# A projection by seven products: sums kept in PSUM banks, two scan levels made a step earlier, and branch B's gate path moved

## The chip, the core and the metric

The kernel runs on one core of one Trainium2 chip. The time is device microseconds of one execution; 1358.66 us is the median of three runs, which lie between 1352.6 and 1362.07. The core's engines work side by side, each through its own queue in order: PE (matmuls; its weight loads are shown as PEld), VectorE (DVE), ScalarE (ACT), GpSimd (POOL) and SyncE (SP), which issues nearly all DMAs. PE writes to eight PSUM banks; here a `[P, 512]` tile of float32 is one bank.

## What is computed

One inference step of one layer for 128 context and 1024 latent tokens (1152 in all) of width 1024. All matmuls of weights are made in three parts (high x high, high x low, low x high) to keep float32 precision.

```python
proj = h @ w_in
q, ff, fb, vi, zA, u, zB, gA, gB = jnp.split(proj, SPLITS, axis=-1)
...
logf_f, k_f = forget_gate(heads(ff), lb_f)
logf_b, k_b = forget_gate(heads(fb), lb_b)
o_f, S_f = hgrn2_chunk_scan(qh, logf_f, k_f, vh, s0_f)
o_b_rev, S_b = hgrn2_chunk_scan(qh[:, ::-1], logf_b[:, ::-1], k_b[:, ::-1], vh[:, ::-1], s0_b)
o = o_f + o_b_rev[:, ::-1]
o = o * lax.rsqrt(jnp.mean(o * o, axis=-1, keepdims=True) + EPS)
o = o * gnorm_w.reshape(N_HEADS_A, HEAD_V)
yA = o.reshape(B, L, D_A) * jax.nn.silu(zA)

yF = jnp.fft.fft2(ug, axes=(1, 3), norm='ortho').real.reshape(B, L, D_B)
yB = yF * jax.nn.silu(zB)
merged = jax.nn.sigmoid(gA) * (yA @ w_pa) + jax.nn.sigmoid(gB) * (yB @ w_pb)
return merged @ w_o, S_f, S_b
```

The scan is `S_t = diag(f_t) S_{t-1} + k_t v_t^T`, `o_t = S_t^T q_t`, for 8 heads and both directions. The context's final states are an output; the latents start from given states.

## The kernel before

**Stages.** From 0 to 174 us: normalisation, modulation, the first gate columns and half of the value projection. From 174 to 887 us: the other projections, as 27 calls of `pair`. From 887 to 1200 us: the scans of 8 heads, with late value columns and then the projection of the branches (`dense`) as filling. Then the last of those products and the output projection.

**`pair` (L613).** One call makes two blocks of 128 output columns for all 1152 tokens by a scheme with seven products instead of eight: `mov[i]` are seven sets of token operands (the halves `h1`, `h2` and the sums `tm`), `w[i]` seven weights, made of the four blocks a11, a21, a12, a22 of `raw` by four sums on VectorE (`sa`). Each weight is cast on ScalarE and its rest taken on VectorE or POOL (`split`). For each half j of 288 columns every product gets a PSUM bank of its own (`any_ps`, six banks in turn) and 12 matmuls, and VectorE forms the results by seven adds (L634) on `m1`, a copy by ScalarE (L647), through `u1`, `u2`, `u3`. `evac` applies the gate function, and a DMA stores the result. `raw` is one buffer, so the next pair's weights are fetched when the last reader is done.

**`four`.** Between products `next(four)` makes a step of other work: `fourier` (4 groups), then `pieces`, which prepares the scan: for each of 16 pieces of a head (640 or 512 tokens), levels of 1, 2 and 4 tokens. A level copies what it needs to `k0` and `q` (`halves`, ScalarE), multiplies `kk`, `qq` and `ff` by the decay (`grow`, VectorE, L461 and L463), makes 32x32 products of tokens (`within`, PE, L481) and merges them. `px` holds `ff` and `qq`, `pz` holds `kk`, `q` and `k0`; both have one buffer, and the next piece is loaded after the last level.

**Scans.** `PATTERN` (L53) has a row for each step n and writes down by hand the order in which parts are emitted: E is `scan_blocks(n)` (levels 8 and 16 of head n), L is `scan_rest(n - 1)` (levels 32 and 64, transposes of `kk`, state, read-out and scaling of the head before), Y the last part of the head before that, F a product of `dense`, V one of the late value columns. Matmuls of this stage are tied to that order (`queued`). All other instructions, and all of the stages before, are ordered by a scheduler when the program is built; each engine then runs its queue in order.

The order of the pairs is written out: two for u, 16 for the heads, seven for gates (`g_dr`), and last two for zB (`silu_fourier`), which need the Fourier result `yf` in tiles that take the place of `px` and `pz`. Then head 0 is loaded into the same place (`load_head`).

Of the kernel before, what the change touches and what calls it, by code (L numbers as in the profile page):

```python
# [11 lines left out]
F32 = mybir.dt.float32  # L12
# [3 lines left out]
ALU = mybir.AluOpType  # L16
# [50 lines left out]
def diffusion_step(ctx: ExitStack, tc: tile.TileContext, xT, x_tok, w_pr, w_v, w_ada, w_ada_gt,  # L67
# [134 lines left out]
    def mm3(out, pairs, mm=nc.tensor.matmul, first=True, last=True):  # L202

        n = len(pairs)
        for i, (sh, sl_, mh, ml) in enumerate(pairs):
            mm(out, lhsT=sh, rhs=mh, start=first and i == 0, stop=False)  # L206
            mm(out, lhsT=sh, rhs=ml, start=False, stop=False)  # L207
            mm(out, lhsT=sl_, rhs=mh, start=False, stop=last and i == n - 1)  # L208
# [350 lines left out]
    def pieces():  # L559
# [6 lines left out]
        def load(hd, t0, t1):  # L566
            w = t1 - t0
            nc.sync.dma_start(x[:, 0, :2 * w].rearrange("p (d t) -> p d t", d=2), f_dr[hd, :, :, t0:t1])
            nc.sync.dma_start(z[:, 1, :w], q_dr[hd, :, t0:t1])

        load(*todo[0])
        for i, (hd, t0, t1) in enumerate(todo):
# [10 lines left out]
            for m in (0,) + EARLY:  # L583
                if m:
                    halves(kk, k0, m, w)
                    halves(qq, q, m, w)
                    grow(ff, kk, qq, m, w)
# [3 lines left out]
                if m == EARLY[-1]:  # L591
                    nc.scalar.copy(fa, ff.rearrange("p (d t) -> p d t", d=2)[:, :, 0:w:GRAN])
                    nc.sync.dma_start(kk_dr[hd, :, :, t0:t1], kk.rearrange("p (d t) -> p d t", d=2))
                    nc.sync.dma_start(qq_dr[hd, :, :, t0:t1], qq.rearrange("p (d t) -> p d t", d=2))
                    nc.sync.dma_start(fa_dr[hd, :, :FA].rearrange("p (d t) -> p d t", d=2)[:, :, t0 // GRAN:t1 // GRAN], fa)
                    nc.sync.dma_start(fa_dr[hd, :, FA + t0 // P * 32:FA + t1 // P * 32], sm_[:, :n * 32])
                    if i + 1 < len(todo):
                        load(*todo[i + 1])
                yield
# [3 lines left out]
    with pool("se", 1) as se, pool("sl", 1) as sl_, pool("sp", 1) as sp:  # L603

        def split(src, tag):
            p = sl_ if tag in ("a12", "a22", "s4") else sp
            hi, lo = (p.tile([P, 4, P], F32R, name=tag + x) for x in "hl")
            nc.scalar.copy(hi, src)  # L608
            eng = nc.vector if tag[0] == "s" else nc.gpsimd
# [3 lines left out]
        def pair(n, evacs):  # L613
# [4 lines left out]
            sa = sp.tile([P, 4, P], F32, name="sa")  # L618
            (a11, a21), (a12, a22) = [[raw[:, 4 * d:4 * d + 4, i * P:(i + 1) * P] for i in range(2)] for d in range(2)]
            w = {1: split(a11, "a11")}  # L620
            nc.vector.tensor_tensor(out=sa, in0=a21, in1=a22, op=ALU.add)  # L621
            w[5] = split(sa, "s1")
            nc.vector.tensor_tensor(out=sa, in0=sa, in1=a11, op=ALU.subtract)
            w[6] = split(sa, "s2")
            nc.vector.tensor_tensor(out=a21, in0=a11, in1=a21, op=ALU.subtract)
            w[7] = split(a21, "s3")
            w[2] = split(a12, "a12")
            w[4] = split(a22, "a22")
            nc.vector.tensor_tensor(out=sa, in0=a12, in1=sa, op=ALU.subtract)
            w[3] = split(sa, "s4")  # L630
            mov = {1: h1[:4], 2: h1[4:], 3: h2[4:], 4: tm[3], 5: tm[0], 6: tm[1], 7: tm[2]}

            def add(out, x, m):
                nc.vector.tensor_tensor(out=out, in0=m, in1=x, op=ALU.add)  # L634

            for j in range(2):
                js = slice(j * SW, (j + 1) * SW)
                m = {}
                for i in (1, 5, 6, 7, 4, 2, 3):
                    m[i] = any_ps()[:, :SW]  # L640
                    mm3(m[i], [(w[i][0][:, k, :], w[i][1][:, k, :], mov[i][k][0][:, js], mov[i][k][1][:, js])
                               for k in range(4)])
                    if i in (() if n < 3 else (5, 4) if n < 8 else (5, 7, 2)):
                        next(four, None)
                m1, u1, u2, u3 = (se.tile([P, SW], F32, name=x) for x in ("m1", "u1", "u2", "u3"))
                ca, cb = (se.tile([P, 2, SW], F32, tag="c", name="c", bufs=3) for _ in range(2))
                nc.scalar.copy(m1, m[1])  # L647
                add(u1, m1, m[6])
                add(u2, u1, m[7])
                add(cb[:, 1], u2, m[5])  # L650
                add(u3, u1, m[5])
                add(ca[:, 0], m1, m[2])
                add(cb[:, 0], u2, m[4])
                add(ca[:, 1], u3, m[3])
                for c, (evac, dst) in zip((ca, cb), evacs):
# [50 lines left out]
        for _ in four:  # L706
            pass
# [450 lines left out]
```

## Time and profile before

| | |
|---|---|
| median of 3 runs | 1358.66 us (1352.6 to 1362.07) |
| profiled execution | 1363.05 us, span 1361.3 us, granted PE clock 0.971 |
| busy share of the span | PE 93%, PEld 87%, DVE 68%, ACT 44%, POOL 35% |
| matmuls | 12768 |

A line of the profile names the line of the code, the engine, the operation and the tiles as out<-in. Idle time in front of an instruction is put down to what released it. A wait "PE x <- DVE y" means that PE stood still, with all that is queued behind, until VectorE's instruction y had ended. "issue" is time for which the profile shows no release.

### The profile page before, as it was taken

The page shows a single profiled execution, that of the slowest core. Times are in us where ns is not written, and L with a number is a line of the kernel's source. Part 1 is how long each engine was busy: PE and PEld are TensorE (multiplying, and loading weights), DVE is VectorE, ACT ScalarE, POOL GpSimd, SP SyncE. Part 2 cuts the span into 40 slices and gives each one's busy share as a digit, 9 for nine tenths or more (in the row PEclk, how much of TensorE's full clock was granted, in tenths as well). Part 3 has the DMA queues.
Part 4 walks back from the last instruction along what each step waited for, and adds up shares of the span by engine and source line. Part 5 has one row for each costly group of instructions (what it writes and reads, how often), then busy time and mean ns, then how long its engine had stood idle before and what let it go on. Part 6 is the DMA issues. An engine that isn't in the chain of part 4 may idle for free.

```text
span 1361.3 us, 31510 instructions
## 1 busy us (share of the span) xinstructions
PE 1260.5 (93%) x12768; PEld 1183.7 (87%) x12768; DVE 922.2 (68%) x1639; ACT 601.3 (44%) x1168; POOL 470.0 (35%) x359
## 2 busy tenths in 40 slices
PE   5899799999999898999999899978999889999998
PEld 3679799999998898899999899977888788999886
DVE  7737755545468878889878787547767676565554
ACT  4542223433445455555554444334655555532332
POOL 4516523142422212122111111632422254455564
PEclk7899899999999999899999999989999899999999
DMA  8542233334445445454554456474776655567342
GB/s 321 197 171 71 66 128 102 132 130 133 134 136 164 148 162 161 155 182 140 179 203 137 166 183 210 142 285 149 236 240 225 217 184 153 169 202 224 113 138 98
DMA packets 126164, 227.54 MB, mean 167 GB/s; under 512 B 15537, under 2 KB 78786, under 8 KB 121794
## 3 DMA queue, kind: packets, MB, share of 16 engines
q1 hardware_dynamic: 125730, 224.47, 49.4%
q8 instruction: 100, 1.64, 0.5%
q10 hardware_dynamic: 288, 1.05, 0.3%
q14 instruction: 46, 0.38, 0.1%
HBM read 153.64 MB, written 71.84 MB: 166 GB/s over the span
## 4 chain that ended last, share of the span: by engine, by line
PE 28%; DMA 9%; DVE 7%; issue 3%; ACT 3%; POOL 2%; SPq 1%; DVEq 0%; ACTq 0%; POOLq 0%
PE d_ps L197 6%; PE o_ps L197 5%; DMA raw<-in_w_pr 3%; PE o_ps L208 3%; PE o_ps L207 3%; PE o_ps L206 3%; DMA wr<-in_w_o 3%; PE o_ps L200 1%; PE d_ps L206 1%; PE d_ps L208 1%; DVE kk L461 1%; PE d_ps L207 1%; DMA qq<-qq_dr 1%; DVE qq L461 1%; POOL a12l L610 1%
## 5 line engine op out<-in xcount | busy, mean ns | idle before, releaser
L183 POOL TENSOR_TENSOR w_lo<-w_raw,w_hi 128x512 fp32r<-128x512 f32 (+1 forms) x36 | 72.2, 2004 | 143.1 <-ACT w_hi L181 136.5
L610 POOL TENSOR_TENSOR a11l<-raw,a11h 128x512 fp32r<-128x512 f32 x27 | 38.5, 1426 | 206.2 <-ACT a11h L608 150.5
L197 PE MATMUL d_ps<-yh,w_hi 128*128 128x288 f32 x256 | 82.8, 323 | 4.4 <-ACT yh L876 2.5
L669 POOL TENSOR_TENSOR c<-c,sg 128x576 f32<-128x576 f32 x24 | 36.3, 1514 | 140.4 <-ACT sg L667 81.1
L197 PE MATMUL d_ps<-yl,w_hi 128*128 128x288 f32 x256 | 76.9, 300 | 1.1 <-POOL yl L877 1.1
L610 POOL TENSOR_TENSOR a22l<-raw,a22h 128x512 fp32r<-128x512 f32 x27 | 39.0, 1443 | 112.5 <-ACT a22h L608 112.5
L197 PE MATMUL d_ps<-yh,w_lo 128*128 128x288 f32 x256 | 76.9, 301 | 0.8 <-POOL w_lo L183 0.8
L893 POOL TENSOR_TENSOR merged<-merged,gs 128x288 f32<-128x288 f32 x64 | 55.1, 872 | 61.5 <-DVE gs L892 59.8
L461 DVE TENSOR_TENSOR qq<-qq,fa 128x1152 f32<-128x1152 f32 x32 | 45.3, 1427 | 23.3 <-ACT qm L467 13.0
L667 ACT ACTIVATE sg<-c 128x576 f32<-128x576 f32 x40 | 27.4, 685 | 73.6 <-DVE c L634 70.1
L610 POOL TENSOR_TENSOR a12l<-raw,a12h 128x512 fp32r<-128x512 f32 x27 | 41.8, 1549 | 51.8 <-ACT a12h L608 44.6
L621 DVE TENSOR_TENSOR sa<-raw 128x512 f32<-128x512 f32 x27 | 20.5, 758 | 57.8 <-DMA raw<-in_w_pr 56.3
L461 DVE TENSOR_TENSOR pz<-pz,px 128x640 f32<-128x640 f32 (+1 forms) x48 | 47.5, 990 | 15.1 <-ACT pz L467 14.8
L634 DVE TENSOR_TENSOR c<-o_ps,u 128x288 f32<-128x288 f32 x108 | 48.5, 449 | 10.8 <-PE o_ps L208 10.3
L181 ACT CAST w_hi<-w_raw 128x512 fp32r<-128x512 f32 (+1 forms) x48 | 34.8, 725 | 47.2 <-DMA w_raw<-in_w_pab 15.3
L197 PEld LDWEIGHTS d_ps<-yh,w_hi 128*128 128x128 f32 x256 | 49.5, 193 | 5.8 <-ACT yh L876 2.7
L467 ACT COPY pz<-pz 128x640 f32<-128x640 f32 (+1 forms) x48 | 37.7, 785 | 33.8 <-PE s_ps L481 22.3
L461 DVE TENSOR_TENSOR kk<-kk,fa 128x1152 f32<-128x1152 f32 x32 | 50.9, 1608 | 0.7
L197 PEld LDWEIGHTS d_ps<-yl,w_hi 128*128 128x128 f32 x256 | 49.8, 194 | 1.3 <-POOL yl L877 1.3
L481 PEld LDWEIGHTS s_ps<-pz 128*32 128x32 f32 x2304 | 26.2, 113 | 27.9 <-issue 20.1
L197 PEld LDWEIGHTS d_ps<-yh,w_lo 128*128 128x128 f32 x256 | 49.4, 193 | 1.1 <-POOL w_lo L183 1.1
L481 PE MATMUL s_ps<-pz 128*32 128x32 f32 x2304 | 33.1, 200 | 16.4 <-issue 8.7
(412 smaller groups left out, 5129.8 us busy)
## 6 DMA issues: line engine op xcount, KB each, us to landing
raw<-in_w_pr SPq DMA_DIRECT2D x52, 512.0 KB, 4.2
gs<-g_dr SPq DMA_DIRECT2D x96, 144.0 KB, 4.3
w_raw<-in_w_pab SPq DMA_DIRECT2D x44, 256.0 KB, 3.1
f_dr<-c SPq DMA_DIRECT2D x32, 288.0 KB, 3.4
kk<-kk_dr SPq DMA_DIRECT2D x8, 1152.0 KB, 5.4
qq<-qq_dr SPq DMA_DIRECT2D x8, 1152.0 KB, 11.1
wa<-in_w_ada SPq DMA_DIRECT2D x8, 1024.0 KB
g_dr<-c SPq DMA_DIRECT2D x28, 288.0 KB, 3.1
```

The lines of the kernel that those rows point to most:

```text
L183: eng.tensor_tensor(out=lo, in0=raw, in1=hi.bitcast(F32), op=ALU.subtract)
L197: queued(nc.tensor.matmul(*args, **kw))
L206: mm(out, lhsT=sh, rhs=mh, start=first and i == 0, stop=False)
L207: mm(out, lhsT=sh, rhs=ml, start=False, stop=False)
L208: mm(out, lhsT=sl_, rhs=mh, start=False, stop=last and i == n - 1)
L461: nc.vector.tensor_tensor(out=xv, in0=xv, in1=view(ff, off, [[2 * mg, n], [step, 2], [0, m]]), op=ALU.mult)
L467: nc.scalar.copy(km.rearrange("p (b i m) -> p b i m", i=2, m=m), view(x, 0, [[2 * m, w // (2 * m)], [w + m, 2], [1, m]]))
L481: mm(ps[32 * j:32 * j + 32, c * 32:c * 32 + 32], lhsT=km[:, ts], rhs=qm[:, ts], start=True, stop=True)
L610: eng.tensor_tensor(out=lo, in0=src, in1=hi.bitcast(F32), op=ALU.subtract)
L634: nc.vector.tensor_tensor(out=out, in0=m, in1=x, op=ALU.add)
L669: nc.gpsimd.tensor_tensor(out=c, in0=c, in1=sg, op=ALU.mult)
L893: nc.gpsimd.tensor_tensor(out=out, in0=out, in1=gs, op=ALU.add)
```

## The change

In `pair`, products share banks. `PRODUCTS` sets their order 1, 5, 6, 2, 7, 4, 3, and both halves j of a product follow each other. Bank "a" takes 1, then 6, 7 and 4 are added to it by the matmuls themselves; bank "d" takes 5 and then 3; bank "b" takes 2. After 1, 6 and 7 ScalarE copies the running sum (x1, x6, x7); three adds by VectorE and one copy for each half give the four results. Weights come from five rotating pairs of tiles. `pieces` makes a level's matmuls one step later than the work that produces their operands, so that a step holds the matmuls of one level and the copies and multiplications of the next; the next piece's f and q are loaded by separate calls. A piece has four steps, not five, and a pair calls `next(four)` five times up to pair 12 and then four times, not four and then six.

The pairs of zB stand ahead of the last two gate pairs; `load_head` for head 0 is emitted between them. In the scans levels 32 and 64 belong to `scan_blocks`, on `s` banks, and hand over `att` and `tot` (now two buffers each); a read-out's reciprocal and scaling are emitted after the next read-out (`scaled`). `PATTERN` is written anew. The weights' layout follows the new order of pairs.

```diff
+PRODUCTS = (1, 5, 6, 2, 7, 4, 3)
+GATES = 6
-PATTERN = ['VVVVVVVVEVVE', 'LVVELVVLEVVLVVLVVLFLFLFLF'] + 6 * ['LFEYLFYLFYELFLFLFLFLFL'] + ['LFYLFYLFYLFLFLFLFLFLF', 'YFYFYFF']
+PATTERN = (['VEVVEVVEVVEVV', 'VEVLVVLEVVLVVLEVVLVVLELFLF'] + 6 * ['EYLFYLEYLFLEFFFLEFLFLF'] +
+           ['YLFYLFYLFLFFFLFLFLF', 'YFYFYFFF'])
...
-            for m in (0,) + EARLY:
-                if m:
-                    halves(kk, k0, m, w)
-                    halves(qq, q, m, w)
-                    grow(ff, kk, qq, m, w)
+            for m, m2 in zip((0,) + EARLY, EARLY + (0,)):
                 ps = scan_ps()
                 within(ps, k0, q, n, nc.tensor.matmul)
                 merge(a32, m, ps, n)
+                if m2:
+                    halves(kk, k0, m2, w)
+                    halves(qq, q, m2, w)
+                    grow(ff, kk, qq, m2, w)
...
+            def keep(i, j):
+
+                x[i, j] = se.tile([P, SW], F32, tag=f"x{i}", name=f"x{i}", bufs=2)
+                nc.scalar.copy(x[i, j], ps["a", j])
...
+            for i in PRODUCTS:
+                bank = {5: "d", 3: "d", 2: "b"}.get(i, "a")
+                for j in range(2):
+                    js = slice(j * SW, (j + 1) * SW)
+                    if i in (1, 5, 2):
+                        ps[bank, j] = any_ps()[:, :SW]
+                    mm3(ps[bank, j], [(w[i][0][:, k, :], w[i][1][:, k, :], mov[i][k][0][:, js], mov[i][k][1][:, js])
+                                      for k in range(4)], first=i in (1, 5, 2), skip_group_check=True)
+                    if i in (1, 6, 7):
+                        keep(i, j)
+                    if i == 2:
+                        result(0, 0, j, 1, "b")
+                    elif i == 7:
+                        result(1, 1, j, 7, "d")
+                    elif i == 4:
+                        result(1, 0, j, None, "a")
+                        done(1, j)
+                    elif i == 3:
+                        result(0, 1, j, 6, "d")
+                        done(0, j)
+                if i in (() if n < 3 else (5, 6, 2, 7, 3) if n < 13 else (5, 2, 7, 3)):
+                    next(four, None)
...
         for j in range(1, KT):
+            if j == GATES:
+                for _ in four:
+                    pass
+                yfs = [lp.tile([P, 2, T], F32, tag=t, name="yfs") for t in ("kk", "qq")]
+                for g in range(0, NG, 2):
+                    pair(n, ((silu_fourier(g), yb_dr[g]), (silu_fourier(g + 1), yb_dr[g + 1])))
+                    n += 1
+                first = load_head(lp, 0, ("kk", "qq", "tab"))
             pair(n, ((sigmoid, g_dr[0, j]), (sigmoid, g_dr[1, j])))
...
+        def scaled(g, ps, on):
+            sg = ss[:, 3 * g:3 * g + 3]
+            nc.vector.reciprocal(sg, sg)
+            nc.vector.tensor_tensor(out=on, in0=ps[:, :TW].rearrange("p (c v) -> p c v", v=P),
+                                    in1=sg.unsqueeze(2).broadcast_to([P, 3, P]), op=ALU.mult)
+            ons.append(on)
...
-            nc.vector.reciprocal(sg, sg)
...
+            if g:
+                scaled(g - 1, *last)
+            last = ps, on
             yield
+        scaled(2, *last)
```

Three places in the built order. First PE, in a pair with pieces. Before, products 7 (operand t2) and 4 (t3) of one half follow each other in banks of their own:

```order
L206 MATMUL o_ps_4505<-t2h3_836,s3h_4243 128x288
L207 MATMUL o_ps_4505<-t2l3_837,s3h_4243 128x288
L208 MATMUL o_ps_4505<-t2h3_836,s3l_4244 128x288
L206 MATMUL d_ps_4523<-t3h0_819,a22h_4251 128x288
L207 MATMUL d_ps_4523<-t3l0_820,a22h_4251 128x288
```

Now product 4 goes into the bank `d_ps_4682` that product 7 has used; ahead of it PE has part of the next pair's product 1 (operand h1, bank 5085) and a piece's matmuls:

```order
L209 MATMUL o_ps_5085<-h1h2_132,wh_5038 128x288
L210 MATMUL o_ps_5085<-h1l2_133,wh_5038 128x288
L211 MATMUL o_ps_5085<-h1h2_132,wl_5039 128x288
L484 MATMUL s_ps_4031<-pz_3607 32x32 x16
L209 MATMUL d_ps_4682<-t3h0_819,wh_4673 128x288
L210 MATMUL d_ps_4682<-t3l0_820,wh_4673 128x288
```

What stood directly behind product 7 now stands behind other matmuls, in a bank that ScalarE must have copied.

Second ScalarE, around the start of a piece (L579, now L585, the first work on a new piece). Before:

```order
L608 CAST s2h<-sa 128x512
L608 CAST a22h<-raw 128x512
L663 ACTIVATE c<-c 128x576
L608 CAST a12h<-raw 128x512
L579 ACTIVATE pz<-px,ones 128x512 x2
L608 CAST s4h<-sa 128x512
L663 ACTIVATE c<-c 128x576
L647 COPY m_9049<-o_ps 128x288
L467 COPY pz<-pz 128x640
```

Now:

```order
L646 COPY x_8411<-d_ps 128x288
L646 COPY x_8425<-o_ps 128x288
L585 ACTIVATE pz<-px,ones 128x512 x2
L618 CAST wh<-raw 128x512
L646 COPY x_8501<-d_ps 128x288
L618 CAST wh<-s_8636 128x512
L470 COPY pz<-pz 128x512
L470 COPY pz<-px 128x512
L618 CAST wh<-s_8637 128x512
L646 COPY x_8517<-o_ps 128x288
```

The copies of running sums stand between the casts and the pieces' copies. Third PE in the scans, from the levels of 32 and 64 (`qq,kk`) to the transposes of the same head's `kk` (`ident,kk`). Before:

```order
L197 MATMUL o_ps<-qq,kk 32x32 x36
...
L197 MATMUL s_ps<-qm,km 32x32 x36
L200 MATMUL o_ps<-ident,on 128x128 x3
L197 MATMUL o_ps<-qq,kk 64x64 x18
...
L200 MATMUL o_ps<-ident,on 128x128 x3
L200 MATMUL o_ps<-ident,kk 128x128 x8
```

Now:

```order
L200 MATMUL o_ps<-vt,kt_sb 128x128 x8
L200 MATMUL s_ps<-qq,kk 32x32 x36
...
L200 MATMUL s_ps<-qq,kk 64x64 x18
...
L200 MATMUL s_ps<-qm,km 32x32 x36
L203 MATMUL o_ps<-ident,on 128x128 x3
L203 MATMUL o_ps<-ident,kk 128x128 x8
```

At each "..." before stand the 12 matmuls of one product of `dense`; now 36 of them and one read-out before level 64, and 36 and two read-outs before the transposes.

More of the change, by code (lines that the diff above doesn't have):

```diff
@@ L200, in transpose, with mm3 @@
         queued(nc.tensor.transpose(*args, **kw))
-    def mm3(out, pairs, mm=nc.tensor.matmul, first=True, last=True):
+    def mm3(out, pairs, mm=nc.tensor.matmul, first=True, last=True, **kw):
         n = len(pairs)
         for i, (sh, sl_, mh, ml) in enumerate(pairs):
-            mm(out, lhsT=sh, rhs=mh, start=first and i == 0, stop=False)
-            mm(out, lhsT=sh, rhs=ml, start=False, stop=False)
-            mm(out, lhsT=sl_, rhs=mh, start=False, stop=last and i == n - 1)
+            mm(out, lhsT=sh, rhs=mh, start=first and i == 0, stop=False, **kw)
+            mm(out, lhsT=sh, rhs=ml, start=False, stop=False, **kw)
+            mm(out, lhsT=sl_, rhs=mh, start=False, stop=last and i == n - 1, **kw)
     with pool("st", 1, side="right") as st, pool("st2", 2, side="right") as st2:
@@ L564, in pieces, with load_f, load_q @@
         todo = [(hd, t0, t1) for hd in range(NH) for t0, t1 in PIECES]
-        def load(hd, t0, t1):
+        def load_f(hd, t0, t1):
             w = t1 - t0
             nc.sync.dma_start(x[:, 0, :2 * w].rearrange("p (d t) -> p d t", d=2), f_dr[hd, :, :, t0:t1])
-            nc.sync.dma_start(z[:, 1, :w], q_dr[hd, :, t0:t1])
-        load(*todo[0])
+        def load_q(hd, t0, t1):
+            nc.sync.dma_start(z[:, 1, :t1 - t0], q_dr[hd, :, t0:t1])
+        load_f(*todo[0])
+        load_q(*todo[0])
         for i, (hd, t0, t1) in enumerate(todo):
@@ L617, in pair @@
                 (nc.scalar if n == 1 else nc.sync).dma_start(raw[:, ks], w_pr[n][:, ks])
-            sa = sp.tile([P, 4, P], F32, name="sa")
+            s1, s2 = (sp.tile([P, 4, P], F32, name=x) for x in ("s1", "s2"))
             (a11, a21), (a12, a22) = [[raw[:, 4 * d:4 * d + 4, i * P:(i + 1) * P] for i in range(2)] for d in range(2)]
[L620 to L623, printed above, removed]
@@ L636, in pair, with weights @@
[L636 to L655, printed above, removed]
-                    evac(c, j)
-                    nc.sync.dma_start(dst.rearrange("p (h j t) -> p h j t", h=2, j=2)[:, :, j, :], c)
+            def weights(i):
+                if i in (1, 2, 4):
+                    return split({1: a11, 2: a12, 4: a22}[i], nc.gpsimd)
+                out, x, y, op = {5: (s1, a21, a22, ALU.add), 6: (s2, s1, a11, ALU.subtract),
+                                 7: (a21, a11, a21, ALU.subtract), 3: (s2, a12, s2, ALU.subtract)}[i]
+                nc.vector.tensor_tensor(out=out, in0=x, in1=y, op=op)
+                return split(out, nc.vector)
@@ new lines, in pair, with result @@
+            mov = {1: h1[:4], 2: h1[4:], 3: h2[4:], 4: tm[3], 5: tm[0], 6: tm[1], 7: tm[2]}
+            w = {i: weights(i) for i in PRODUCTS}
+            ps, x, cs = {}, {}, {}
+            def keep(i, j):
+                x[i, j] = se.tile([P, SW], F32, tag=f"x{i}", name=f"x{i}", bufs=2)
+                nc.scalar.copy(x[i, j], ps["a", j])
+            def result(b, h, j, i, bank):
+                if (b, j) not in cs:
+                    cs[b, j] = se.tile([P, 2, SW], F32, tag="c", name="c", bufs=4)
+                c = cs[b, j]
+                if i is None:
+                    nc.scalar.copy(c[:, h], ps[bank, j])
+                else:
+                    nc.vector.tensor_tensor(out=c[:, h], in0=ps[bank, j], in1=x[i, j], op=ALU.add)
@@ L703, in diffusion_step @@
         for j in range(1, KT):
+            if j == GATES:
[6 more added lines that the diff above has]
+                first = load_head(lp, 0, ("kk", "qq", "tab"))
             pair(n, ((sigmoid, g_dr[0, j]), (sigmoid, g_dr[1, j])))
             n += 1
-        for _ in four:
-            pass
-        yfs = [lp.tile([P, 2, T], F32, tag=t, name="yfs") for t in ("kk", "qq")]
-        for g in range(0, NG, 2):
-            pair(n, ((silu_fourier(g), yb_dr[g]), (silu_fourier(g + 1), yb_dr[g + 1])))
-            n += 1
-        first = load_head(lp, 0, ("kk", "qq", "tab"))
         tstack.close()
@@ L770, in scan_rest @@
                        rhs=qq[:, 1 - j % 2, t1:t1 + 32], start=True, stop=True)
+        grow(fa, kk2, qq2, 32, g=GRAN)
         for j in range(4):
@@ L1125, in _layout @@
     for j in range(1, KT):
+        if j == GATES:
+            names += [("zB", g) for g in range(NG)]
         names += [("gA", j), ("gB", j)]
-    names += [("zB", g) for g in range(NG)]
     w_pr = blocks(np.concatenate([blk[k][:, i] for k, i in names], 1), 2 * P)
```

74 lines of the change are left out of this document (32 added, 42 removed).

## The prediction

> **What bounds the kernel now.** I read first the table of stretches, because shares over the whole span mix stages with different limits. Its columns are the stretch, its length, then busy time and instruction count of PE, PEld, DVE, ACT and POOL, then the mean granted clock, the DMA share and GB/s.
>
> ```profile
> 174.50:222.00 47.50, 47.50 (x359) 47.50 (x358) 25.44 (x51) 11.96 (x22) 16.93 (x14) 1.00 0.39 124
> 222.00:404.00 182.00, 181.89 (x1307) 175.53 (x1307) 90.53 (x180) 72.25 (x136) 52.23 (x44) 1.00 0.40 133
> 404.00:836.00 432.00, 406.01 (x4966) 389.71 (x4965) 357.72 (x611) 222.97 (x366) 88.01 (x57) 0.98 0.49 161
> 836.00:887.00 51.00, 51.00 (x385) 51.00 (x384) 32.38 (x52) 16.88 (x31) 28.91 (x20) 1.00 0.60 203
> 887.00:945.00 58.00, 43.97 (x671) 42.14 (x670) 35.50 (x47) 24.21 (x36) 17.70 (x10) 0.88 0.59 210
> 945.00:1170.00 225.00, 200.94 (x2979) 192.76 (x2978) 153.39 (x309) 124.19 (x319) 84.64 (x63) 0.97 0.64 207
> ```
>
> The first four are the 27 projection pairs: plain, with the Fourier branch, with the scan's pieces, plain again. The last two are the scans. Where nothing disturbs it (836 to 887), PE starts a matmul of 288 columns each 51.00 / 385 = 0.1325 us. The same table for the pieces' matmuls alone (L481) says what else PE does from 404 to 836.
>
> ```profile
> 404.00:836.00 432.00, 33.06 (x2304) 26.25 (x2304) 0.98 0.49 161
> ```
>
> So there 4966 - 2304 = 2662 large matmuls need 352.7 us at that pace and the small ones 33.1, together 385.8; **46 us of the 432 are lost**, some 2.9 for each of the 16 pieces. By the busy column only 432.00 - 406.01 = 26 would be lost. The Trainium skill says of this ("Perfetto Trace Analysis", section "Identifying the Most-Contended Engine") that matmul busy time is a bad measure of how near the limit one is, since matmuls are pipelined. By the busy column the projections' terms below would come to 26 / 46 x 32 = 18 us in place of 32; the pace of the undisturbed row bears the rule out, and the sum goes by the pace.
>
> What PE waited for there is in its waits (engine, line, releaser: us in total, times, longest):
>
> ```profile
> PE s_ps L481 <- issue: 8.7, 9, 1.9
> PE d_ps L206 <- DVE u L634: 6.1, 5, 2.1
> PE s_ps L481 <- ACT pz L467: 4.7, 8, 0.9
> PE o_ps L206 <- DVE u L634: 3.4, 2, 1.8
> PE s_ps L481 <- DVE pz L581: 2.9, 1, 2.9
> ```
>
> Two kinds: a product waits for a bank that VectorE's sums have not emptied (9.5), and a piece's small matmuls wait for operands from VectorE and ScalarE (16.3). VectorE is 357.72 / 432 = 83% busy there, runs in order, and waits itself for transfers:
>
> ```profile
> DVE sa L621 <- DMA raw<-in_w_pr: 25.3, 12, 4.3
> DVE px L580 <- DMA pz<-q_dr: 14.2, 10, 3.2
> ```
>
> In the scans PE waited for this (887 to 1200):
>
> ```profile
> PE o_ps L200 <- DVE kk L461: 14.6, 7, 4.7
> PE o_ps L197 <- DVE kk L461: 4.5, 4, 1.8
> PE d_ps L197 <- DVE vo L922: 4.2, 2, 3.6
> PE s_ps L197 <- ACT qm L467: 3.8, 1, 3.8
> PE o_ps L197 <- issue: 3.0, 1, 3.0
> PE d_ps L197 <- ACT yh L876: 2.5, 1, 2.5
> PE d_ps L197 <- issue: 1.5, 1, 1.5
> PE s_ps L197 <- issue: 1.3, 1, 1.3
> PE d_ps L197 <- POOL yl L877: 1.1, 1, 1.1
> ```
>
> Together 36.5 us, over half of them behind one thing: `grow` multiplying `kk` for levels 32 and 64, which the next matmuls of the same head read.
>
> **The projections' sums.** A pair had 14 adds on VectorE and 2 copies on ScalarE; now it has 6 adds, and 8 copies (x1, x6, x7 and one result, for each half).
>
> ```profile
> L634 DVE TENSOR_TENSOR c<-o_ps,u 128x288 f32<-128x288 f32 x108 | 48.5, 449 | 10.8 <-PE o_ps L208 10.3
> L647 ACT COPY m<-o_ps 128x288 f32<-128x288 f32 x21 | 8.1, 384 | 0.0
> ```
>
> VectorE loses 8 x 0.449 = 3.6 us a pair, ScalarE gains 6 x 0.384 = 2.3. Neither engine is the bound, so these are not subtracted; what counts is the slack. From 404 to 836 there are 2662 / 168 = 15.8 pairs: VectorE goes from 22.6 to 19.0 us a pair, ScalarE from 14.1 to 16.4, against 24.4 us (385.8 / 15.8) of PE. Matmuls keep their number. Banks: a pair took 14, each waiting for its turn among VectorE's sums; now it takes 6. The 9.5 us of waits for `DVE u` go.
>
> The new wait is PE's own: products 6, 7 and 4 may be added into bank "a" only after ScalarE has copied it. Behind that wait stands all of PE's queue. Between product 1 and 6, and 6 and 7, of one half lie three other half products, 3 x 12 x 0.1325 = 4.8 us; between 7 and 4 one, 1.6 us, and what the order puts there besides: often part of the next pair's product 1 and a piece's small matmuls, as shown above. A copy needs 0.384 and a hand-over at each end. The chain of waits shows one, from a product's last matmul to VectorE's sum and on to ScalarE:
>
> ```profile
> 886.97 0.14 PE o_ps L208
> 887.13 0.47 DVE c L634
> 887.69 0.69 ACT sg L667
> ```
>
> The sum starts 0.02 us after the matmul's slot, ScalarE 0.09 after the sum. So 1.6 us cover a copy (0.6 with both hand-overs) and one instruction ahead of it on ScalarE, not three. No such wait is in this trace; below it is bounded by nothing (always covered), above by the 1.8 of the longest wait for an emptied bank, twice a pair over 27 pairs, 97 us. I take 4 us, 0.15 a pair, near the lower end, since ScalarE is at 67% and other work stands in between.
>
> **Weights.** Seven pairs of tiles become five that rotate; a product's weights are made while the four before it run, 4 x 3.2 = 12.7 us ahead. Before, the next pair's raw block could be fetched only when a12 was split, which waited for product 2 of the second half, near the pair's end. Now the last reads wait for products 1 and 5 of the same pair, so the fetch starts early in it, while VectorE's first use of the block stands behind the adds of product 2, past the pair's middle: some 8 us later, over the 4.9 to 6.9 us that these fetches take in the chain.
>
> ```profile
> 657.81 5.36 DMA raw<-in_w_pr
> 820.01 6.94 DMA raw<-in_w_pr
> ```
>
> The 25.3 us of VectorE's waits go, worth nothing by themselves, but they stand ahead of the pieces' sums in its queue.
>
> **Pieces.** A level's matmuls now come one step after the work that makes them, five steps a pair at first, then four, against six. With 3.6 us less work and 25.3 / 15.8 = 1.6 less waiting a pair, I take two thirds of the 16.3 us of operand waits away, 11. The remaining 46 - 25.8 = 20 us are refilling after each wait and the lower clock (0.98); they go with the waits, (9.5 + 11) / 25.8 = 0.8, so 16. **Projections: 9.5 + 11 + 16 - 4 = 32 us.** The Fourier stretch has no listed PE wait: nothing.
>
> **Gate path of branch B.** The two pairs move ahead of the last two gate pairs, so the pieces must end before: in SP's queue the four loads of `yfs` wait for the pieces' last matmuls, and the next raw block stands behind them; on POOL the two products with `yfs` stand ahead of the next splits. A pair is 24 us and the pieces' matmuls end a quarter of the way into the second of them, so I count nothing, at most 4 (one such fetch) if late. What goes is the end of the stage, four multiplications on POOL and then the first head's load:
>
> ```profile
> 888.45 1.70 POOL c L669
> 893.12 1.41 POOL c L689
> 895.12 11.35 DMA qq<-qq_dr
> 906.55 1.16 ACT qm L467
> ```
>
> That load now runs under two pairs. PE had 30 us of late V work beside it, so it gains only its waits: 3.8 (`ACT qm`) and 2 of the 4.2 (`DVE vo`).
>
> **Scans.** Levels 32 and 64 are computed in the step before. Ahead of level 64 there now stand 36 of `dense`'s matmuls instead of 12, ahead of the transposes again 36 and two read-outs instead of 12; 36 x 0.1325 = 4.8 us and more, against 1.43 + 1.61 us for `grow`:
>
> ```profile
> L461 DVE TENSOR_TENSOR kk<-kk,fa 128x1152 f32<-128x1152 f32 x32 | 50.9, 1608 | 0.7
> L461 DVE TENSOR_TENSOR qq<-qq,fa 128x1152 f32<-128x1152 f32 x32 | 45.3, 1427 | 23.3 <-ACT qm L467 13.0 <-PE o_ps L197 10.1
> DVE ss L841 <- ACT ss L840: 41.7, 19, 4.8
> ```
>
> The 19.1 us of `kk` waits go. Scaling a step later takes most of the 41.7 us that VectorE stood before its reciprocals; it holds one bank of four a step longer. Of the change from branch B's to branch A's projection (3.0, 2.5, 1.5, 1.1) I take 5. What is late next is VectorE: 153.39 / 225 = 68%, 74% if the stretch shrinks by 18. New waits at its tail: between 0 and the 19.1 they replace; I take 8, 1 us a head. **Scans: 3.8 + 2 + 19.1 + 5 - 8 = 22.** Start and end of the kernel are untouched.
>
> **Sum.** 32 + 22 = 54; the profiled execution took 1363 us, 4 above the median shown and inside its spread, so 1309 and, seen from the median, **1307**.
>
> **Rivals.** *The waits move but stay (1336, 0.20).* The pieces' chain (copy, multiply, copy, matmul) is in order on three engines, and ScalarE now has the copies in its queue. Then only the bank waits (9.5), 2 of refill and two thirds of the scans' term (15) go: 27. For it: 8.7 us of "issue" show nothing that the change removes.
>
> *Nothing net (1353, 0.11).* The scheduler's order does not fit the real times of fetches, as today's 25.3 us show, and new waits take all but 10.
>
> *ScalarE's hand-backs decide (1388, 0.07).* PE stops at products 6, 7 and 4 until ScalarE has copied. At 1.5 us for each half of product 4, two a pair, 27 pairs, it costs 81, so 1307 + 81. It decides from 54 / 54 = 1 us a hand-back. Two sigmoids (0.69) ahead of a copy are enough. Against it: other work stands between. The Trainium skill has a rule for this ("Perfetto Trace Analysis", section "Matmuls"): independent groups should rotate through banks, so that emptying one overlaps the next. Here the trace shows only rotation, with 9.5 us of waits all the same.
>
> *Everything goes (1278, 0.07).* 46 + 36.5, and a little.
>
> **Numbers.** The forecast holds 0.55. The range goes from 1279 to 1343: down to nearly all waits gone, up past the second case. About 1% (14 us) is what a measurement can tell from no change. Faster by more: 0.55 + 0.07 + 0.20 = 0.82; within: 0.11; slower: 0.07.
>
> **What would show it.** In the changed profile: no PE wait for `DVE` at a product's first matmul; the stretch with pieces some 400 us long, PE's waits for s_ps under 8 us; VectorE's wait for raw under 8 us; no waits of PE for `kk`; the first head's matmuls right at the scan's start. I am wrong if PE waits for ScalarE's x copies by over 20 us, or if the scan stretch keeps its 313 us.

## The result: 1% faster

The changed kernel took **1345.69 us** (median of 5; 1345.08 to 1348.67), the kernel before 1359.45 (median of 5 beside it): ratio 0.9895, 95% interval 0.9872 to 0.9918. Forecast were 1307 and a range of 1279 to 1343, so the direction was right and the gain about a quarter of the forecast. The profiled execution took 1346.88 us, its span is 1345.1, granted clock 0.978.

The stages of the changed kernel, in the columns of the table of stretches shown above (length; PE, PEld, DVE, ACT, POOL busy; clock, DMA share, GB/s), then the pieces' matmuls alone (L484, once L481):

```profile
215.00:398.00 183.00, 183.00 (x1317) 177.08 (x1318) 74.26 (x126) 85.32 (x176) 54.40 (x46) 1.00 0.40 136
398.00:826.00 428.00, 401.81 (x4938) 381.99 (x4937) 312.19 (x485) 252.97 (x459) 89.90 (x59) 0.99 0.46 157
826.00:894.00 68.00, 62.84 (x468) 62.14 (x467) 28.04 (x41) 27.44 (x56) 32.46 (x23) 1.00 0.67 240
894.00:945.00 51.00, 45.74 (x768) 43.93 (x766) 37.48 (x58) 28.73 (x49) 8.54 (x6) 0.93 0.55 177
945.00:1152.00 207.00, 193.69 (x2870) 186.62 (x2869) 151.19 (x300) 115.95 (x311) 74.52 (x60) 0.98 0.68 218
...
398.00:826.00 428.00, 32.64 (x2304) 25.87 (x2304) 0.99 0.46 157
```

The first pair starts at 175.5, so the projections take 718.5 us; before, 174.5 to 887, 712.5. **Forecast -32, measured +6.** The scans go from 894 to 1183, 289 us after 313. **Forecast -22, measured -24.** By the same reckoning as before, 2634 large matmuls at 0.1325 us and 32.6 make 381.6 of the 428, and 46 us are lost, as many as before. VectorE has 45 us less to do (357.7 to 312.2) and ScalarE 30 more, both less than was worked out (57 and 36 for 15.8 pairs); it bought nothing.

PE's waits there (engine, line, releaser: us in total, times, longest) have other names and are split finer; all listed ones together are 25.8, as before:

```profile
PE s_ps L484 <- issue: 4.0, 5, 1.2
PE s_ps L484 <- DVE pz L587: 3.7, 4, 1.8
PE s_ps L484 <- ACT pz L470: 3.4, 4, 1.3
PE s_ps L484 <- DMA pz<-q_dr: 3.3, 2, 1.9
PE o_ps L211 <- POOL wl L619: 2.5, 4, 0.8
PE d_ps L209 <- DVE c L656: 2.3, 6, 0.7
PE d_ps L209 <- ACT x L646: 1.8, 2, 1.3
PE o_ps L209 <- ACT x L646: 1.7, 5, 0.5
...
PE o_ps L209 <- DVE c L656: 0.9, 1, 0.9
```

The products' waits for VectorE's sums fell from 9.5 us (`DVE u`) to 3.2 (`DVE c`), and the hand-backs of the x copies cost 3.5. The pieces' matmuls still wait 14.4 after 16.3, now also for a load, and products wait for their weights (`POOL wl`). VectorE and ScalarE in the same stretch:

```profile
DVE pz L587 <- ACT pz L585: 31.1, 7, 6.3
DVE px L586 <- DMA pz<-q_dr: 30.4, 7, 6.9
...
DVE s L636 <- DMA raw<-in_w_pr: 11.2, 8, 2.2
```

```profile
ACT pz L585 <- DMA px<-f_dr: 54.5, 15, 4.5
ACT wh L618 <- DVE s L636: 34.1, 17, 3.9
ACT wh L618 <- DMA raw<-in_w_pr: 24.0, 12, 3.5
```

VectorE's waits for raw weights did fall (25.3 to 11.2). But ScalarE now stands 24 us for them directly, which it did not before, and 34 for the sum that VectorE makes of them, against 8.1 (`s2h <- DVE sa`). In the scans the picture is the forecast one (894 to 1183): the 19.1 us behind `kk` are 2.5, all PE waits together 18.5 in place of 39.1 (the lines that the prediction added up to 36.5 leave out four short ones). The longest:

```profile
PE d_ps L200 <- ACT yh L911: 2.8, 1, 2.8
PE o_ps L203 <- ACT kt_sb L832: 2.7, 2, 2.5
PE s_ps L200 <- DVE kk L464: 2.5, 1, 2.5
PE d_ps L200 <- DVE fa L466: 2.5, 3, 1.5
```

### The profile page after: what moved, and what is told of

It is laid out like the page before. It is cut to its first block, busy times and chain, and to the rows that moved or that the text cites. A ratio compares the mean times of both kernels' runs of the same rounds, so it can differ in the third digit from the quotient of the medians.

```text
span 1345.1 us, 31341 instructions
## 1 busy us (share of the span) xinstructions
PE 1257.2 (93%) x12768; PEld 1176.5 (87%) x12768; DVE 842.7 (63%) x1423; ACT 650.8 (48%) x1330; POOL 459.0 (34%) x359
## 3 DMA queue, kind: packets, MB, share of 16 engines
q10 hardware_dynamic: 288, 1.05, 0.3%
## 4 chain that ended last, share of the span: by engine, by line
PE 52%; DVE 18%; DMA 16%; ACT 5%; issue 5%; SPq 2%; POOL 1%; DVEq 0%; ACTq 0%; POOLq 0%
PE d_ps L200 6%; DMA raw<-in_w_pr 6%; PE o_ps L209 6%; PE o_ps L210 6%; PE d_ps L209 6%; PE o_ps L211 5%; PE d_ps L210 5%; PE d_ps L211 5%; PE o_ps L200 5%; DMA qq<-qq_dr 2%; DVE s L636 2%; DVE px L464 2%; DMA pz<-q_dr 2%; DVE pz L464 2%; DVE ts L432 1%
## 5 line engine op out<-in xcount | busy, mean ns | idle before, releaser
L619 POOL TENSOR_TENSOR wl<-raw,wh 128x512 fp32r<-128x512 f32 x81 | 115.8, 1430 | 465.4 <-ACT wh L618 418.4
L619 DVE TENSOR_TENSOR wl<-s,wh 128x512 fp32r<-128x512 f32 x81 | 62.7, 777 | 80.4 <-ACT wh L618 80.2
L209 PE MATMUL o_ps<-h1h,wh 128*128 128x288 f32 x324 | 97.1, 300 | 3.7 <-DVE c L656 2.0
L211 PE MATMUL o_ps<-h1h,wl 128*128 128x288 f32 x324 | 96.4, 298 | 2.5 <-POOL wl L619 2.5
L618 ACT CAST wh<-raw 128x512 fp32r<-128x512 f32 x108 | 66.4, 616 | 64.6 <-DMA raw<-in_w_pr 42.9
L210 PE MATMUL o_ps<-h1l,wh 128*128 128x288 f32 x324 | 96.8, 299 | 0.0
L618 ACT CAST wh<-s 128x512 fp32r<-128x512 f32 x81 | 50.2, 620 | 88.3 <-DVE s L636 43.7
L209 PEld LDWEIGHTS o_ps<-h1h,wh 128*128 128x128 f32 x324 | 61.1, 189 | 5.1 <-ACT wh L618 2.4
L211 PEld LDWEIGHTS o_ps<-h1h,wl 128*128 128x128 f32 x324 | 60.9, 188 | 3.8 <-POOL wl L619 3.5
L210 PEld LDWEIGHTS o_ps<-h1l,wh 128*128 128x128 f32 x324 | 61.0, 188 | 0.5 <-issue 0.3
L696 POOL TENSOR_TENSOR c<-c,sg 128x576 f32<-128x576 f32 x24 | 39.1, 1629 | 37.9 <-ACT sg L694 35.7
```

Source lines behind the costliest of these rows:

```text
L209: mm(out, lhsT=sh, rhs=mh, start=first and i == 0, stop=False, **kw)
L210: mm(out, lhsT=sh, rhs=ml, start=False, stop=False, **kw)
L619: eng.tensor_tensor(out=lo, in0=src, in1=hi.bitcast(F32), op=ALU.subtract)
L696: nc.gpsimd.tensor_tensor(out=c, in0=c, in1=sg, op=ALU.mult)
```

## Which part did what

**scans_only**: the kernel before with the new `scan_blocks`, `scan_rest` and `PATTERN`.

> The kernel before with the changed scans alone (levels 32 and 64 in scan_blocks, scaling a step later, new PATTERN); projections, pieces and gate path as before. If the parts add up as the two traces show them (scans 313 to 289 us, projections 712.5 to 718.5), the scans alone give 1359 - 24 = 1335 us, 10 below the changed kernel; the stretch with pieces keeps its 432 us. If the scans gained only because head 0 is loaded earlier (gate path moved), it gives some 1350.

Measured 1349.42, ratio 0.9896 (0.9879 to 0.9914): the scans alone give what the whole change gives, not 24 us. Their stretch is 297 us (887 to 1184). What is missing stands in one row of PE's waits:

```profile
PE s_ps L198 <- ACT qm L468: 18.6, 1, 18.6
```

The new `PATTERN` begins head 0 after one late V column instead of eight, so the load of head 0 lies open. That is what the moved gate path is for; I had priced it only by the old wait of 3.8. So the 16 us by which the scans are shorter here (297 after 313) hold a new wait of 15 us more.

**proj_only**: the changed kernel with the old scans.

> The changed kernel with the scans of before: PSUM sums, re-stepped pieces and moved gate path only. My prediction's own term (-32) would give 1327; the trace of the changed kernel says +6 less what the earlier load of head 0 gains (up to 6), so 1359 to 1366.

Measured 1358.39, ratio 0.9964 (0.994 to 0.9989): the projections and the gate path are worth some 5 us. In the trace that is two things. The projections are 8 us longer than before (720.5). The old scans are some 15 shorter (895 to 1193.5, 298 us in place of 313): what reaches into them is the gate path, which loads head 0 earlier, and PE's wait for `ACT qm` is gone. So the gate path, forecast to gain 5.8 us in the scans, gains 15 with the old ones. The two parts, 1.0% and 0.4%, add up to a little more than the whole's 1.05%; both act on the scans' start.

**zb_last**: the changed kernel with the block under `if j == GATES:` (the pairs of zB, head 0's load) behind the loop of the gate pairs again.

> The changed kernel with the pairs of zB and head 0's load last, as before. With the old projections the moved gate path cost 12 us in the comparison (1363 beside 1349), since the zB pairs waited for the pieces' end; here pieces end at 825 of 894 and PE lost 5 to 6 us behind it. If the moved path gains 8 at the scan's start and loses 5: 1347 to 1351. If it loses more than it gains here too: 1335 to 1343, and the rest of the projections' part is worth more than the comparison with all of it says.

Measured 1349.61, ratio 0.9907 (0.9879 to 0.9935), beside 0.9895: not to be told from the changed kernel. The projections are 4 us shorter (714.4), the scans 8 longer (296.7), with PE's wait at their start back (16.7 for `ACT qm`). So with the new scans the moved path gains 8 us and costs 4.

**scans_gates**: the moved gate path on the old projections, with the new scans.

> The kernel before with the changed scans and the moved gate path, projections and pieces as before. The scans alone gave a ratio of 0.990 (-12 us of its trace: 887 to 1184 in place of 1200). The changed kernel's scan stretch is 289, 8 shorter than 297. If that comes from head 0 being loaded ahead of the last two pairs, this kernel gives another -8 less what PE loses behind the pieces' end (some 5): ratio 0.984 to 0.988, time some 1341 beside 1361 for the kernel before. If it is worth nothing: 0.990. If old pieces end too late for it (they ran to 836 of 887) and the zB pairs wait: above 0.993.

Measured 1363.33, ratio 1.0017 (0.9996 to 1.0038): against scans_only the moved path costs some 14 us here and eats the scans' gain. PE, behind the end of the old pieces, and VectorE there:

```profile
PE o_ps L208 <- DVE c L636: 15.2, 1, 15.2
```

```profile
DVE c L636 <- DMA yb_dr<-c: 16.4, 2, 13.3
```

VectorE's sum waits for a result buffer (`c`) that goes out, to `yb_dr`, only when the zB pairs have `yf`, whose place the pieces still hold; the granted clock from 829 to 909 is 0.87. So the mechanism that I bounded at 4 us costs 15 where pieces end late. In the changed kernel PE waits 5.1 us at this place, in zb_last 1.2.

**scale_now**: the changed kernel with each read-out scaled at once.

```diff
-            if g:
-                scaled(g - 1, *last)
-            last = ps, on
+            scaled(g, ps, on)
             yield
-        scaled(2, *last)
```

> The changed kernel with each read-out scaled at once, as before. If the deferral carries the scans' gain: back by 8 to 15 us, 1354 to 1361. If the levels made a step earlier carry it (19.1 us of PE's waits for kk): same as the changed kernel within 4 us, 1342 to 1350.

Measured 1346.99, ratio 0.9866 (0.9842 to 0.989): the deferral is worth nothing. What is left for the scans' gain are the levels made a step earlier, in step with the `kk` waits that went, and the new `PATTERN`; no run parts these two.

## Where the projections' 32 us went

First I took the queue for the cause.

**raw_pool** (`raw` fetched through POOL's queue) and **piece_pool** (the pieces' DMAs through it):

```diff
-                (nc.scalar if n == 1 else nc.sync).dma_start(raw[:, ks], w_pr[n][:, ks])
+                (nc.scalar if n == 1 else nc.gpsimd).dma_start(raw[:, ks], w_pr[n][:, ks])
```

> The changed kernel with the weights' raw blocks fetched through POOL's queue in place of SP's, where they stand behind the pieces' stores and loads. Theory one loop (on SP the second half of raw waits behind the piece's stores and f load; ScalarE's copies for the piece wait behind the casts that need raw, so piece and weights hold each other up, some 3 us in each of 16 pieces): DVE's wait s <- raw (11 us) and ScalarE's wh <- raw (24 us) mostly go, the stretch with pieces falls from 428 to 385-400, time 1310 to 1325. Theory piece chain alone (load f, 1 - f, copies, multiplications, stores, each after the other with one px and one pz, some 27 us whatever the weights do): 428 stays within 5, time 1340 to 1350. Theory fetches themselves too slow: the waits for raw stay.

> The changed kernel with all DMAs of pieces (f, q, kk, qq, fa) through POOL's queue; raw stays on SP. Theory one loop: the same gain as with raw on POOL, 1310 to 1325, unless POOL's splits now wait behind the pieces' loads, which would show as POOL idle before wl. Theory piece chain alone: 1340 to 1350, or worse by what POOL's queue adds.

Measured 1356.83 (0.9957, 0.9937 to 0.9977) and 1360.91 (0.9997, 0.9977 to 1.0017): both slower than the change. So taking the blocks, or the pieces, out of SP's queue does not help. VectorE's wait in raw_pool rose:

```profile
DVE s L636 <- DMA raw<-in_w_pr: 35.6, 14, 3.3
```

The Trainium skill ("SBUF — State Buffer", section "Who interferes with whom") says that a DMA that seems stalled by a VectorE operation is one issued by GpSimd, and that a `tensor_tensor`, which is most of what VectorE runs here, did not stall one. This case shows no such stall in the fetches: the median one there took 4.5 us from issue to landing, 5.8 in the changed kernel. What moved is the order: VectorE's sum of a block starts 5.3 us behind the issue of the block's second half, 7.2 in the changed kernel (means over 16 pairs).

Then I took the transfers away altogether.

**no_fetch** (weights fetched for three pairs only), **no_load** (f and q for the first piece only), **neither** (both left out):

```diff
+        kept = []
...
-            raw = sp.tile([P, KT, 2 * P], F32, name="raw")
-            for d in range(2):
+            if n <= 3:
+                kept.append(sp.tile([P, KT, 2 * P], F32, name="raw"))
+            raw = kept[-1]
+            for d in range(2 if n <= 3 else 0):
```

> The changed kernel, but pairs from the fourth on take their weights from the block that the third has fetched (24 fetches of raw and their waits left out; the output is another). Fixed price theory (of the 46 us lost in the stretch with pieces some 19 are the 64 changes of PE from large to small matmuls and back, 0.3 us each as the trace shows, and only the 26 to 30 of listed waits can go): stretch not below 400. If late raw blocks are behind those waits: PE's listed waits fall from 25.8 us to under 8, stretch 402 to 408, time some 1325. If the pieces' own chain is: waits stay above 18, stretch 418 to 428, time 1338 to 1346.

> The changed kernel, but f and q are loaded for the first piece only (30 loads left out, later pieces work on what is in the buffers; the output is another). If the pieces' own chain (store, load f, 1 - f, ... in one px and one pz) makes the waits, its period of 27 us gets 5 to 6 us shorter, under the 24.1 us of PE's work for a pair with a piece: PE's listed waits fall from 25.8 us to under 10, stretch 400 to 410, time some 1325. If late weights make them: waits above 18, stretch 418 to 428.

> Both left out together: raw fetched three times only, f and q loaded once. If transfers that come late are behind all listed waits, whichever it is, stretch 400 to 404 (the large matmuls' 349, the small ones' 33 and the 64 changes' 19), time 1315 to 1322. If waits come from the order in which PE's queue was built, which fits the engines' real times no better without transfers: listed waits still above 12 us, stretch above 412.

Measured 1306.00 (0.959, 0.9558 to 0.9621), 1320.43 (0.9688, 0.9655 to 0.9721) and 1313.52 (0.9646, 0.961 to 0.9682). Without fetches the stretch takes 392 us, and PE has one wait left in it:

```profile
397.00:789.00 392.00, 388.68 (x4914) 375.31 (x4913) 311.56 (x482) 257.09 (x456) 88.17 (x59) 1.00 0.40 132
```

```profile
PE s_ps L484 <- issue: 3.2, 5, 1.0
```

The projections take 680 us, 32 fewer than before. In the other two the pieces end at 754 and 729 us, so that their stretches hold fewer pairs and only the whole projections compare: 695 and 686. So either transfer's absence helps, by 38 and by 24 us of the 718.5: the two loops hang together, and the block is the larger part. (The operand waits do not tell them apart: 10.7 us are left without the pieces' loads, and 9.7 with the blocks gone as well.) How a block can hold up a piece, one of the changed kernel shows (start, us, engine, line, tiles; in brackets the idle time ahead and its releaser; ScalarE, then VectorE, then PE):

```profile
619.07 0.62 ACT L618 CAST wh<-raw 128x512 fp32r<-128x512 f32 x1 [1.87 <-DMA raw<-in_w_pr]
619.59 0.39 ACT L646 COPY x<-d_ps 128x288 f32<-128x288 f32 x1
621.68 0.62 ACT L618 CAST wh<-s 128x512 fp32r<-128x512 f32 x1 [1.70 <-DVE s L636]
622.21 1.03 ACT L470 COPY pz<-pz 128x640 f32<-128x640 f32 x1
```

```profile
618.46 0.82 DVE L587 TENSOR_TENSOR pz<-pz 128x640 f32<-128x640 f32 x1
...
620.43 1.17 DVE L636 TENSOR_TENSOR s<-raw 128x512 f32<-128x512 f32 x1 [0.42 <-DMA raw<-in_w_pr]
```

```profile
619.38 0.55 PE L484 MATMUL s_ps<-pz 128*32 128x32 f32 x40 [0.96 <-issue]
```

The piece's sum (`pz`, L587, its `k0`) is done at 619.28, and the small matmuls that read it at 619.93. From then on the copy for the next level could write `k0` anew. The copy (L470) starts at 622.21, because the cast `wh<-s` stands ahead of it on ScalarE, and that waits for VectorE's sum of a block that has just landed. A piece that ends late puts off its next load too; how often that happens was not counted.

**before_no_fetch**: the same 24 fetches left out of the kernel before.

> The kernel before with 24 of its 27 fetches of raw left out in the same way (pairs from the fourth on use the third's block; the output is another). If the late block holds up the old projections as it does the new ones, and the PSUM sums are worth nothing by themselves: projections 712 to some 680, as in the changed kernel without fetches (680), time some 1328. If the sums in PSUM free PE of waits for emptied banks (9.5 us listed before) and of operand waits, it keeps them: projections 690 to 700, PE still waits for DVE u, time 1337 to 1347. If the old projections have another bound (VectorE 83% busy in the stretch): projections above 700.

Measured 1384.10, ratio 1.0141 (1.0117 to 1.0165): the last of the three cases, though I had not expected it to be slower (projections 734 us). The stretch takes 446 us, and PE waits for the pieces' operands much more than it did with the fetches:

```profile
PE s_ps L481 <- ACT pz L467: 21.9, 16, 2.6
PE s_ps L481 <- issue: 15.5, 9, 2.4
PE s_ps L481 <- DVE pz L581: 7.5, 3, 3.5
```

VectorE itself stands there for the next piece's load, 14.2 us before and now:

```profile
DVE px L580 <- DMA pz<-q_dr: 73.0, 15, 5.9
```

So the two kernels differ in their bound. In the old one the pieces' own chain, with its load behind the last level, comes late without the fetches too; why it is even slower than with them is not shown (the build orders the work otherwise). In the new one this bound is gone (392 against 446 us). Sums in PSUM, the step between operands and matmuls and the earlier load of `f` can each have a part in that; no run parts them. What is left in the new one is mostly the block.

**twice**: no_fetch with the small matmuls of every level issued two times in a row.

> The changed kernel without fetches (no_fetch, 1306), and the small matmuls of each of the 64 levels of pieces issued twice in a row into the same bank (same values as once). If each change between large and small matmuls has a price (0.09 us on the last large one, 0.11 on the last small, 0.10 on the first large one), the number of changes is the same and only the matmuls are added: 0.35 to 0.4 us for each of 64, some 24 us, and the number of large matmuls that take 0.06 us or more too long stays near 122. If the delay belongs to the small matmuls themselves or to their operands, it doubles: 45 us or more.

Measured 1333.51, 27.5 above no_fetch; by the traces the projections are 22.6 longer (702.4 and 679.8, first to last pair). The stretch:

```profile
396.00:797.00 401.00, 396.08 (x7112) 381.83 (x7111) 311.56 (x476) 250.15 (x446) 91.36 (x55) 1.00 0.39 131
```

2504 large ones at 0.1325 make 331.8, so the small ones with all around them take 69.2; in no_fetch 2610 make 345.8 and leave 46.2. Twice the small matmuls cost 23 us more, 0.36 for each of the 64 levels, and the other 23 do not depend on their number: 3.2 are listed waits in no_fetch, the rest, 20 us or 0.3 a level, is a price of going from large matmuls to small ones and back. (The stretch of no_fetch fell below the 400 that I had set as its floor, since the busy share of the small matmuls, 32.6, already holds 10 of these 20 us.)

**early_free**, **half_double**, **early_half**: real repairs, one by one and together.

```diff
-                                 7: (a21, a11, a21, ALU.subtract), 3: (s2, a12, s2, ALU.subtract)}[i]
+                                 7: (s1, a11, a21, ALU.subtract), 3: (s2, a12, s2, ALU.subtract)}[i]
-            w = {i: weights(i) for i in PRODUCTS}
+            w = {i: weights(i) for i in (1, 5, 6, 2, 4, 7, 3)}
...
-            raw = sp.tile([P, KT, 2 * P], F32, name="raw")
+            raws = [sp.tile([P, 4, 2 * P], F32, name=f"raw{d}", bufs=1 + d) for d in range(2)]
...
-                x[i, j] = se.tile([P, SW], F32, tag=f"x{i}", name=f"x{i}", bufs=2)
+                x[i, j] = se.tile([P, SW], F32, tag="x6" if i == 6 else "x1", name=f"x{i}", bufs=2)
```

> The changed kernel, with weights made in the order 1, 5, 6, 2, 4, 7, 3 and the sum of product 7 written to s1 in place of raw: now all reads of raw fall among the first five of the rotating tiles, so that none waits for product 1 on PE, and the next block can be fetched earlier. Theory late raw block (one raw buffer, freed 8 us into the pair, then SP's queue and a fetch of 6.5 us; ScalarE's and VectorE's waits for it hold up the pieces behind them): the fetch is issued 4 to 8 us earlier, PE's listed waits in the stretch with pieces fall from 25.8 to 8-15 us, time 1325 to 1335. Theory transfers as such (raw's packets compete with the pieces' and their mere presence makes both late): no change, 1340 to 1350.

> The changed kernel, with raw as two tiles of half a block, the one of a12 and a22 in two buffers (x1 and x7 share a tag to make room). The half that is freed last no longer stands in the way. Theory late raw block: PE's listed waits from 25.8 to 8-15 us, time 1325 to 1335. Theory transfers as such: 1340 to 1350. If x1 and x7 sharing costs anything, it shows as ScalarE's x copies waiting for VectorE's c.

> Both: weights in the order 1, 5, 6, 2, 4, 7, 3 and the second half of raw in two buffers. Theory late raw block: close to the kernel without fetches (1306; the stretch with pieces 392 there), 1312 to 1325. Theory transfers as such: 1340 to 1350.

Measured 1348.03 (0.9895, 0.9857 to 0.9934), 1350.94 (0.9918, 0.9885 to 0.9951) and **1328.69 (0.9752, 0.9722 to 0.9782)**. Beside the changed kernel each alone is worth nothing, both together 19 us. In early_free VectorE still waits 19.5 us for raw: the fetch's second half is issued 23.2 us ahead of the pair's product 5 instead of 17.2 (means over 16 pairs), but the build has moved VectorE's sum forward too, to 5.4 us behind that issue instead of 7.2. In early_half it waits none at all, though every block is still fetched, and PE's waits for the pieces are down to 0.9 us:

```profile
PE d_ps L209 <- ACT x L645: 5.1, 12, 1.0
PE o_ps L209 <- ACT x L645: 4.9, 4, 2.6
PE s_ps L484 <- issue: 0.7, 1, 0.7
PE s_ps L484 <- ACT pz L470: 0.2, 1, 0.2
```

Its projections are 705 us. Against no_fetch it has these hand-backs of x, and behind the pieces' end the wait of scans_gates is back:

```profile
PE o_ps L209 <- DVE c L655: 10.3, 1, 10.3
```

**early_half_g7**: early_half with `GATES = 7`, the zB pairs ahead of the last gate pair only.

> The kernel early_half (1328.7, ratio 0.975) with GATES = 7: the pairs of zB and head 0's load stand ahead of the last gate pair only, one pair (22 us) later. If PE's 10 us wait behind the pieces' end is the gate path standing too early: it goes, and head 0 (11 us to load) still comes under the last pair: 1317 to 1322, ratio 0.967 to 0.970. If it is a bound of the pairs after the pieces: 1326 to 1331.

Measured **1322.39** (1320.23 to 1323.34), ratio 0.9698 (0.9684 to 0.9711): the fastest of those that leave nothing out, 3% under the kernel before. PE's wait there is 2.0, and at the scans' start 3.4.

## Why the prediction was wrong, step by step

- **What bounds it, half right.** Of the 46 us lost I took 20 for refilling after waits that would go with them. no_fetch, with hardly a wait, still loses 13.6 by that reckoning (392 - 345.8 - 32.6), and by twice 10 of it are fixed. The row of a change (start, duration, line, form):

```profile
564.69 0.29 PE L211 MATMUL d_ps<-t2h,wl 128*128 128x288 f32 x1
564.91 0.56 PE L484 MATMUL s_ps<-pz 128*32 128x32 f32 x40
565.40 0.40 PE L209 MATMUL o_ps<-t2h,wh 128*128 128x288 f32 x1
565.64 0.29 PE L210 MATMUL o_ps<-t2l,wh 128*128 128x288 f32 x1
```

  From the last large matmul to the first small one are 0.22 us, where the next large one would come after 0.133; the first large one afterwards takes 0.24. The Trainium skill ("TensorEngine Tiling (Array Packing)", section "Key Properties") says that changing the tiling mode drains TensorE; these rows fit that and give a price. So some 36 us could go, not 46, and none did. (The prediction's last step also slips by 2 us: 54 below the median of 1358.66 is 1305, not 1307.)
- **The projections' sums, right in the main.** The 9.5 us of bank waits fell to 3.2, and VectorE lost 45 us of work (3.6 x 15.8 = 57 expected). The hand-backs cost 3.5 in the stretch, against 4 taken for all pairs; the 3.1 behind it are not there in zb_last and belong to the gate path.
- **Weights: the step that failed.** I wrote that the fetch now starts early in the pair, some 8 us ahead of VectorE's first use, so that the waits for it go. The 8 us came out (8.0 from the first half's issue to that use, 5.9 before; means over 16 pairs). What I left out is the way from that use to the product: casts, rests and sums on three engines. The traces of one pair, before (SP's issue, VectorE's first use, PE's product 5) and after (POOL's last read of the block before, then the same three):

```profile
630.28 0.81 SPq L617 DMA_DIRECT2D raw<-in_w_pr  x2
```

```profile
635.60 1.45 DVE L621 TENSOR_TENSOR sa<-raw 128x512 f32<-128x512 f32 x1 [0.54 <-DMA raw<-in_w_pr]
```

```profile
655.94 0.30 PE L206 MATMUL o_ps<-t0h,s1h 128*128 128x288 f32 x1
```

```profile
636.12 1.49 POOL L619 TENSOR_TENSOR wl<-raw,wh 128x512 fp32r<-128x512 f32 x1 [0.34 <-POOL c L696]
```

```profile
641.14 0.50 SPq L626 DMA_DIRECT2D raw<-in_w_pr  x1
...
642.84 0.43 SPq L626 DMA_DIRECT2D raw<-in_w_pr  x1
```

```profile
650.85 0.67 DVE L636 TENSOR_TENSOR s<-raw 128x512 f32<-128x512 f32 x1
```

```profile
661.29 0.29 PE L209 MATMUL o_ps<-t0h,wh 128*128 128x288 f32 x1
```

  From VectorE's use to product 5 there are 10.4 us here in place of 20.3 (means over 16 pairs: 10.0 and 18.5), and from the issue of the second half to product 5 the means are 17.2 and 23.8. So the fetch did not start earlier against the work that needs it, but later. Before, weights were made most of a pair ahead, and "near the pair's end" was the end of the pair before. Now product 4's weights come sixth in five rotating tiles and wait for product 1, here until 633.0; then ScalarE's cast and POOL's rest stand behind other work in their queues, and POOL reads raw until 637.6, 8 us into a pair that began at 629.25. SP has the pieces' transfers ahead of the fetch, and the fetch itself takes 5.8 us to land in the median, 4.2 before. I had the release right, but never set the old lead beside the new one. So the waits went from VectorE to ScalarE, which also has the pieces' copies, and the terms that hung on their going (11 us of the pieces' waits, 16 of refilling) did not come: the pieces' waits went from 16.3 to 14.4. That late blocks hold up the stretch is shown by no_fetch (392 us in place of 428) and, with every block still fetched, by early_half. That the shorter lead is what makes them late is argued from these rows and not shown: early_free, with the lead back, gained nothing.
- **Pieces, right only where no block is late.** Without fetches the new code gives just the forecast 32 us (712.5 to 680), and the old code none (734). The equal number is partly luck, since no_fetch takes 24 transfers away as well and keeps the 10 us of fixed price. And this term hung on the one above; I gave both one chance. The rival "the waits move but stay" named what happened; its price still let it keep 12 us of the projections.
- **Gate path, too small on both sides.** Nothing (at most 4) as cost, 5.8 as gain: 4 and 8 in the changed kernel, 14 and 15 with the other half of the code as it was. That the new `PATTERN` needs it (18.6 us in scans_only) I had not seen.
- **Scans, right in sum** (-24 against -22), through the `kk` waits, which went from 19.1 to 2.5. That the sum agrees this well is partly luck, since the new `PATTERN`'s wait and the gate path's larger gain, both unpriced, offset each other. Scaling later was counted as freeing VectorE: its wait before the reciprocals is 30.6 us after 49.3 in the whole of the scans (the 41.7 was a part), and worth nothing.

Open: why early_free and half_double gave nothing alone (in early_free the build moved the use along; for half_double not even that is shown); other orders come with each edit, so differences of some 5 us between them have no single cause that these runs show.

## What to carry to other kernels

Where two loops share engines in order (here weights and pieces), freeing work in one of them may buy nothing while the other's transfer has a single buffer: leave the transfer out once, in both versions, and see which loop is left. When tiles begin to rotate, work out for each fetched buffer who reads it last and how far ahead of the next use that is, in both orders; and ask whether an order built from estimates will move the use forward as soon as the fetch comes earlier.

## What was unexpected in the hardware

Going from 128x288 matmuls to a block of 32x32 products and back costs 0.3 us at both block sizes tried (64 times, 20 us here), and the busy column counts half of that as work. Fetching blocks through POOL's queue left VectorE waiting 35.6 us for them where SP's queue left 11.2, though the transfers landed sooner (4.5 us in place of 5.8): the built order moved VectorE's use forward, so these runs show no price of that queue itself.
